# A diffusion layer with 32 experts: expert biases split behind the router, weight slots given back in two steps, waits moved in the expert loop

## The chip, the cores and the metric

The kernel runs on one core of one Trainium2 chip. TensorE (PE) does the matmuls, VectorE (DVE), ScalarE (ACT) and GpSimd (POOL) the elementwise work, and SyncE (SP) issues most DMAs. The metric is the device time of one execution, in microseconds (us): 1415.83 us before, the median of three runs from 1415.27 to 1415.89.

## The reference

One layer, 256 tokens of 1024 values. An adaLN-modulated bidirectional gated DeltaNet attention over the tokens and a context, then a mixture of 32 experts of which each token takes its best four, then an RMSNorm:

```python
hx2 = modulate(rmsnorm(x, norm2_g), mx[3], mx[4])
logits = hx2 @ w_r + b_r
top_v, top_i = lax.top_k(logits, 4)
comb = one_hot(top_i) weighted with softmax(top_v)
for e in range(32):
    gu = hx2 @ w_gu[e] + b_gu[e]                     # 1024 x 2048
    gate = minimum(gu[:, :1024], 7); up = clip(gu[:, 1024:], -7, 7)
    y += comb[:, e] * ((up + 1) * gate * sigmoid(1.702 * gate) @ w_dn[e] + b_dn[e])
x = x + mx[5] * y
return rmsnorm(x, final_g)
```

(Written shorter than the source.) All values are float32. An expert's weights are 8 MB for `w_gu` and 4 MB for `w_dn`, 402 MB for all 32, and each is read once.

## The kernel before

**Stages.** The attention with the adaLN products runs from 0 to about 420 us; its instructions are put in order by a scheduler from the table `ORDER`, whose entries name operations (`k`, `v`, `q`, `st`, `norm`, `wo`, `op`, `bias`, `issue`). The router follows until about 436.5 us, then the loop over 32 experts until 1406 us, then the last scatter, the norm and the output.

**Weights.** The experts' weights are cut into 192 pieces of 2 MB, six for each expert: four of `w_gu`, each with two of the eight k-steps, and two of `w_dn`. They pass through a ring of nine buffers, called slots. `issue(n)` starts the next n pieces on SP's queue (line 778); a piece can start when the slot that it takes has been read to the end by the matmuls. Nine pieces are issued ahead of the loop (two of them by `issue` in `ORDER`, seven in `issue(NR - NA)`).

**An expert.** Up to 64 tokens are gathered by a one-hot matmul into `hTe` (one gather per pair of experts, `gather4`). `first(e, ks)` does k-steps of the gate and up product: `gemm1` (line 992), started by `gbias` (line 984), a matmul with the expert's row of the bias in three bfloat16 parts (`bgu`, 96 rows: three times 32 experts). Then `swish` on DVE and ACT, `turn` (four transposes into `psT`, line 1010, and a copy to `aT` on ACT, line 1011), `dbias` (line 1018, with `bdn`), and the down product `gemm2r` (line 1025, 32 matmuls). For each pair, `weights` makes the matrix `ST` that scatters the outputs back, and `scatter` (line 1084) adds the pair before to the tokens. PE's order in the loop is the order in which the code is written. Before each `turn` PE runs k-steps 0 and 1 of the next expert.

**Overflow.** An expert with more than 64 tokens takes a second pass over the same weights in a block under `over()`, a branch on a flag that every engine loads after the router (`flag`, line 1122). In this run only expert 9 takes it. There are two such blocks for an expert: after the eight k-steps (line 1174) and after the down product (line 1204). Each is followed by `issue`: four slots after the first (one, one and two at three blocks for expert 0), two after the second. Where the branch isn't taken, SP's wait for a slot lasts until PE is past the branch. Another branch, `many` (line 1090), before expert 28, is for over 128 tokens and loads its number there.

**Biases.** `bias(i)` (line 835) splits a quarter of the biases into three bfloat16 parts, during the attention: casts on DVE (lines 844 and 846), subtracts on POOL (line 847).

Of the kernel before, what the change touches and what calls it, by code (L numbers as in the profile page):

```python
# [25 lines left out]
ORDER = [('k', 0), ('k', 1), ('ada',), ('n', 0), ('dc', 2), ('ada',), ('k', 2), ('dc', 1), ('ada',), ('ada',), ('dc', 0), ('k', 3), ('v', 1), ('um', 0), ('dc', 6), ('um', 1), ('ada',), ('n', 2), ('dc', 3), ('v', 0), ('um', 2), ('um', 3), ('k', 6), ('ia', 0), ('k', 5), ('dc', 5), ('dc', 4), ('k', 4), ('v', 2), ('ada',), ('k', 7), ('ib', 0), ('v', 3), ('n', 4), ('v', 4), ('dc', 7), ('n', 6), ('um', 7), ('um', 5), ('ic', 0), ('um', 6), ('um', 4), ('v', 5), ('ia', 4), ('ada',), ('ada',), ('v', 6), ('st', 0, 0, 0), ('ada',), ('st', 0, 1, 0), ('st', 0, 2, 0), ('v', 7), ('q', 0), ('ada',), ('st', 0, 3, 0), ('ada',), ('q', 1), ('q', 3), ('z', 3), ('am', 0), ('q', 2), ('am', 1), ('q', 6), ('z', 1), ('am', 3), ('ada',), ('ada',), ('am', 2), ('st', 1, 0, 0), ('st', 1, 1, 0), ('st', 1, 2, 0), ('ib', 4), ('ic', 4), ('q', 5), ('q', 4), ('ada',), ('st', 0, 0, 4), ('st', 0, 1, 4), ('st', 0, 2, 4), ('ada',), ('ada',), ('q', 7), ('st', 1, 3, 0), ('st', 0, 3, 4), ('am', 7), ('am', 5), ('z', 2), ('z', 5), ('z', 0), ('am', 4), ('z', 4), ('z', 7), ('z', 6), ('am', 6), ('norm', 0, 1), ('wo', 2), ('st', 1, 0, 4), ('hclose',), ('st', 1, 1, 4), ('g1',), ('moec',), ('norm', 0, 0), ('wo', 6), ('bias', 4), ('wo', 1), ('st', 1, 2, 4), ('issue',), ('wo', 0), ('wo', 3), ('st', 1, 3, 4), ('bias', 5), ('wo', 5), ('norm', 4, 1), ('op', 0, 1), ('issue',), ('op', 0, 0), ('bias', 0), ('wo', 7), ('norm', 4, 0), ('wo', 4), ('op', 4, 1), ('op', 4, 0), ('bias', 2), ('bias', 1), ('bias', 3), ('fin',)]  # L26
# [26 lines left out]
def tile_kernel(ctx: ExitStack, tc: tile.TileContext, A, out):  # L53
# [88 lines left out]
    nc.scalar.dma_start(rowG, A["norm2_g"].rearrange("o (q r) -> (o q) r", q=4))  # L142
# [242 lines left out]
    V.tensor_scalar(neg_eg, eg, -1.0, None, op0=ALU.mult)  # L385

# [414 lines left out]
    mk, bx = {}, []  # L801

    def moec():
# [17 lines left out]
        bx.extend(xp.tile([P, 512], F32, tag=t, name="bx", bufs=1) for t in "gu")  # L821
# [11 lines left out]
    def bias(i):  # L833

        g, n = divmod(i, 2)
        if not n:
            for n_ in range(2):
                b = A["moe_b_dn"][0] if g == 2 else A["moe_b_gu"][0][:, g * D:(g + 1) * D]
                nc.sync.dma_start(bx[n_][32 * g:32 * g + 32], b[:, n_ * 512:(n_ + 1) * 512])
        x = bx[n][32 * g:32 * g + 32]  # L840
        hi = (mk["bdn"] if g == 2 else mk["bgu"][:, g * D:(g + 1) * D])[:, n * 512:(n + 1) * 512]
        sb = wka.tile([P, 512], BF, tag="vT", name="sb", bufs=1)[32 * g:32 * g + 32]
        for u in range(3):
            V.tensor_copy(hi[32 * u:32 * u + 32], x)
            if u < 2:
                V.tensor_copy(sb, x)
                G.tensor_tensor(x, x, sb, op=ALU.subtract)

    ops = {"dc": decu, "moec": moec, "fin": moer, "g1": gates, "bias": bias, "k": key, "n": knorm, "v": value, "um": umats, "ia": inv_a, "ib": inv_b, "ic": inv_c, "st": step, "q": query,
# [29 lines left out]
    fwi = mc.tile([1, 2], I32, name="fwi")  # L879
    xTs = [mw.tile([P, 8, P], F32, tag="hTe", name="xT") for _ in range(2)]  # L880
# [183 lines left out]
    def weights(e, oh):  # L1064

        pt = px()
        for t in range(2):
            T.transpose(pt[:, t * P:(t + 1) * P], oh[:, t].bitcast(F32), ident)
        ST = mw.tile([P, 4, P], FR, tag="ST", name="ST", bufs=1)
# [3 lines left out]
        for t in range(2):  # L1073
            T.matmul(pt[:, 256:260], oh[:, t], chl[:, t, e:e + 2].rearrange("p e w -> p (e w)"), start=(t == 0), stop=(t == 1))
# [12 lines left out]
    def many(p):  # L1087

        n_max = nc.values_load(cnti[0:1, E:E + 1], min_val=0, max_val=256)
# [31 lines left out]
    softmax()  # L1121
    flag = [nc.values_load(fwi[0:1, i:i + 1], min_val=0, max_val=65535) for i in range(2)]
    live = {}

    def first(e, ks):
# [5 lines left out]
        for k in ks:  # L1131
            gemm1(e, k, ws[k], hT[:, k, e % 2 * 64:e % 2 * 64 + 64], pg, pu)

    def beside(e, k):

        nonlocal ST, cw
        if e % 2:
            if e + 1 < E and k in (3, 5):
                nxt = pairs[e // 2 + 1]
                gather4(nxt[0].bitcast(F32), P, nxt[1], k // 4)  # L1140
        elif k == 4 and e:
            for n in range(2):
                for t in range(2):
                    scatter(t, n)
        elif k == 5:
# [6 lines left out]
    for e in range(E):  # L1152
# [11 lines left out]
        for k0, k1 in ((0, 2), (2, 4), (4, 8)) if e == 0 else ((2, 8),):  # L1164
            for k in range(k0, k1):
# [3 lines left out]
            if k0 == 0 or e:  # L1169
                pgo, puo = pb(f"G{1 - odd}"), pb(f"U{1 - odd}")  # L1170
            if k1 == 4:
                S.activation(s2[:, 0, 0:1], epsc, AF.Silu)
            tc.no_sync_barrier()
            with over():
                if k0 == 0 or e:
# [13 lines left out]
        for n in range(2):  # L1189
# [4 lines left out]
        for r in range(8):  # L1194
            gemm2r(r, ws[8 + r], aT, py, e, odd)
        y = xp.tile([P, 512], F32, tag="u", name="y", bufs=1)
        V.scalar_tensor_tensor(y, py, cw[:, odd:odd + 1], gate[:, odd], op0=ALU.mult, op1=ALU.mult)  # L1197
        for half in range(2):
            n = half ^ odd
            r = slice(64 * half, 64 * half + 64)  # L1200
            S.copy(YAB[0][r, n], y[r])  # L1201
# [59 lines left out]
```

## Time and profile before

| | |
|---|---|
| time, median of 3 runs | 1415.83 us (1415.27 to 1415.89) |
| the profiled execution | 1424.81 us |
| its span in the trace | 1423.0 us |
| PE busy | 1270.0 us, 89% |
| DVE, ACT, POOL busy | 501.1, 356.8, 229.6 us |
| mean DMA rate over the span | 321 GB/s |
| DMA rate in most slices of the expert loop | 426 to 428 GB/s |
| PE's clock in the loop, share of full speed | 0.96 to 1.00 |

The profile shows one execution. PE is busy nearly throughout, but a busy engine need not be the bound: in the expert loop the DMA rate stands at one value in most slices, and falls in three: at the loop's start, around 740 us and shortly after 1297 us. The columns of the DMA rate in windows of the trace therefore belong beside PE's busy time. The profiled execution took 8.98 us more than the median of the runs.

### The profile page before, as it was taken

Reading aid. Unit: us, or ns where it says so; the run is one execution under the profiler, and the core shown is the slowest. Engines: PE = TensorE matmul, PEld = TensorE weight load, DVE = VectorE, ACT = ScalarE, POOL = GpSimd, SP = SyncE. Lnnn points to the kernel's source line nnn. Section 1 sums busy time; section 2 is a strip of 40 time slices with the busy share of each in tenths; the row PEclk is TensorE's granted clock in tenths of the full one; section 3 lists DMA queues with packets and bytes.
Section 4 is the critical chain, followed back from the end, with each engine's and each line's share of the span. In section 5 each row is a group of like instructions: output and inputs, shape, how many; then the busy total and the mean of one; then the engine's idle time right before and its main releaser. Section 6 shows DMA issues by size and latency. Waiting matters only on the chain. (4 is left out here: it accounts for less than half of the span.)

```text
span 1423.0 us, 18206 instructions
## 1 busy us (share of the span) xinstructions
PE 1270.0 (89%) x6815; PEld 642.7 (45%) x6815; DVE 501.1 (35%) x1101; ACT 356.8 (25%) x802; POOL 229.6 (16%) x216
## 2 busy tenths in 40 slices
PE   4999889999889999999998999999889899897995
PEld 2576677688544433434333433334334344342432
DVE  4569988866762112021112112121120211212022
ACT  3366443455323111111111111111111111110112
POOL 3043234334430100011000110001000010000011
PEclk9899999989999999999999999999999999999996
DMA  9632433443577899999984999999999999999991
GB/s 257 190 117 81 119 104 105 149 134 115 168 299 313 330 428 425 427 426 426 427 343 191 428 426 426 427 427 426 427 426 426 427 426 427 427 421 378 430 426 51
DMA packets 88432, 456.27 MB, mean 321 GB/s; under 512 B 7892, under 2 KB 57241, under 8 KB 63713
## 3 DMA queue, kind: packets, MB, share of 16 engines
q1 hardware_dynamic: 85680, 454.08, 79.5%
q8 instruction: 93, 1.52, 0.4%
q10 hardware_dynamic: 2609, 0.26, 0.2%
q14 instruction: 50, 0.41, 0.1%
HBM read 453.27 MB, written 1.05 MB: 319 GB/s over the span
## 5 line engine op out<-in xcount | busy, mean ns | idle before, releaser
L992 PE MATMUL psG<-w,hTe 128*64 128x512 f32 x1024 | 282.3, 607 | 30.6 <-DMA w<-in_moe_w_gu_dram 18.2
L992 PE MATMUL psU<-w,hTe 128*64 128x512 f32 x1024 | 277.2, 597 | 0.0
L1025 PE MATMUL psY<-w,aT 128*64 128x512 f32 x1024 | 229.2, 600 | 22.0 <-ACT aT L1011 22.0
L1202 POOL TENSOR_TENSOR YAB<-y,YAB 64x512 fp32r<-64x512 f32 x62 | 79.6, 1283 | 891.7 <-ACT YAB L1201 889.4
L1197 DVE SCALAR_TENSOR_TENSOR y<-psY,cw,gate 128x512 f32<-128x512 f32 x32 | 24.0, 751 | 373.5 <-PE psY L1025 373.5
L992 PEld LDWEIGHTS psU<-w,hTe 128*64 128x64 f32 x1024 | 89.0, 138 | 127.6 <-issue 115.3
L1025 PEld LDWEIGHTS psY<-w,aT 128*64 128x64 f32 x1024 | 71.2, 138 | 159.5 <-issue 129.8
L992 PEld LDWEIGHTS psG<-w,hTe 128*64 128x64 f32 x1024 | 77.6, 137 | 141.3 <-issue 114.3
L1000 DVE TENSOR_SCALAR g<-psG 128x512 f32<-128x512 f32 x33 | 34.4, 1041 | 260.2 <-PE psG L992 260.0
L1201 ACT CAST YAB<-y 64x512 fp32r<-64x512 f32 x64 | 39.4, 616 | 259.2 <-DVE y L1197 137.9
L268 PE MATMUL pp<-hh,w 128*128 128x256 f32 (+1 forms) x240 | 86.2, 373 | 5.9 <-DVE acc L443 4.4
L269 PE MATMUL pp<-hl,w 128*128 128x256 f32 (+1 forms) x240 | 84.8, 367 | 0.0
L977 ACT ACTIVATE hTe<-psX,adac,A 128x128 f32<-128x128 f32 x128 | 48.3, 457 | 116.2 <-PE psX L975 116.2
L83 POOL TENSOR_TENSOR w<-w 128x1024 fp32r<-128x1024 f32 x24 | 57.5, 2396 | 105.6 <-ACT w L78 32.3
L1029 DVE TENSOR_TENSOR x<-x,psX 128x512 f32<-128x512 f32 x68 | 43.9, 685 | 83.0 <-PE psX L1084 81.1
L975 PEld LDWEIGHTS psX<-oh,xn 128*128 128x128 f32 x512 | 59.5, 191 | 25.0 <-issue 25.0
L975 PE MATMUL psX<-oh,xn 128*128 128x128 f32 x512 | 65.4, 281 | 0.6 <-DVE oh L966 0.6
L443 DVE SCALAR_TENSOR_TENSOR acc<-pp,colB,acc 128x508 f32<-128x508 f32 (+3 forms) x96 | 62.4, 653 | 9.4 <-ACT acc L431 8.5
L1011 ACT ACTIVATE aT<-psT 128x512 f32<-128x512 f32 x32 | 19.1, 597 | 157.8 <-PE psT L1010 157.8
L268 PEld LDWEIGHTS pp<-hh,w 128*128 128x128 f32 x240 | 49.8, 208 | 18.5 <-issue 3.6
L269 PEld LDWEIGHTS pp<-hl,w 128*128 128x128 f32 x240 | 50.1, 209 | 6.4 <-issue 1.0
L424 PE MATMUL pp<-hh,w 128*128 128x256 f32 (+1 forms) x240 | 52.3, 349 | 0.0
(394 smaller groups left out, 1458.7 us busy)
## 6 DMA issues: line engine op xcount, KB each, us to landing
w<-in_moe_w_gu_dram SPq DMA_DIRECT2D x128, 2048.0 KB, 24.5
w<-in_moe_w_dn_dram SPq DMA_DIRECT2D x64, 2048.0 KB, 20.2
w<-in_gdn_w_in_dram SPq DMA_DIRECT2D x32, 512.0 KB, 4.0
w<-in_ada_w_dram SPq DMA_DIRECT2D x32, 512.0 KB, 4.0
sl<-in_ada_w_dram SPq DMA_DIRECT2D x16, 512.0 KB, 5.7
w<-in_gdn_w_out_dram SPq DMA_DIRECT2D x8, 512.0 KB
xt<-in_ctx_dram SPq DMA_DIRECT2D x2, 512.0 KB
xt<-in_x_dram SPq DMA_DIRECT2D x2, 512.0 KB
```

The costliest lines, as they stand in the source:

```text
L83: eng[e2].tensor_tensor(lo, x, hi.bitcast(F32), op=ALU.subtract)
L268: T.matmul(ps, wh, xh, start=first, stop=False)
L269: T.matmul(ps, wh, xl, start=False, stop=last and not low)
L424: T.matmul(p[:, t0:512], w[1][:, k], hh[:, k, t0:512], start=False, stop=(k == 7))
L443: V.scalar_tensor_tensor(o, i, tap(j), o, op0=ALU.mult, op1=ALU.add)
L975: T.matmul(pt[:, d % 4 * n:d % 4 * n + n], xn[:, t, d * P:(d + 1) * P], oh[:, t, 0:n], start=(t == 0), stop=(t == 1))
L977: S.activation(dst[:, d, 0:n], pt[:, d % 4 * n:d % 4 * n + n], AF.Identity, scale=A2[:, d:d + 1], bias=B2[:, d:d + 1])
L992: T.matmul(ps[64 * c:64 * c + 64], hc, w[:, q * D + c * 512:q * D + (c + 1) * 512], start=False, stop=(k == 7))
L1025: T.matmul(py[o:o + 64], aT[:, b, c * 64:(c + 1) * 64], w[:, n * 512:(n + 1) * 512], start=False, stop=(r == 7))
L1029: V.tensor_tensor(xs, xs, ps, op=ALU.add)
L1201: S.copy(YAB[0][r, n], y[r])
L1202: (G if e + 1 < E else V).tensor_tensor(YAB[1][r, n], y[r], YAB[0][r, n].bitcast(F32), op=ALU.subtract)
```

## The change

1. `bias` leaves `ORDER`. It is written again behind the router, for three biases instead of six quarters: for each, ACT's queue issues three copies of 128 KB (32 rows of 1024) into a 96-row tile, ACT casts (once 96 rows, three times 32), DVE subtracts twice. Two tiles are used in turn. Expert 0 adds `gbias` behind its last k-step instead of ahead of its first (`late`).
2. The row of `norm2_g` is loaded and transposed at the end of the gates' stage instead of the kernel's start.
3. The block under `over()` behind the k-steps is split in two for each expert (after k-step 3 and after k-step 7), each followed by `issue(2)`; for expert 0 in four, each with `issue(1)`.
4. In the loop: only k-step 0 of the next expert stands ahead of `turn`, k-step 1 and `dbias` behind it; `weights` runs at k-step 6 instead of 5 and puts its small matmuls with `chl` ahead of ACT's casts; `scatter` is halved between k-steps 3 and 5; the odd expert's `gather4` stands at k-steps 2 and 5 instead of 3 and 5.
5. The number for `many` is loaded once, with the flags.
6. For the last expert the second overflow block stands ahead of the down product, and a small Sqrt activation (it brings the function table) behind its `turn`.

```diff
-ORDER = [... ('bias', 4) ... ('bias', 5) ... ('bias', 0) ... ('bias', 2), ('bias', 1), ('bias', 3), ('fin',)]
+ORDER = [... ('fin',)]
...
+    def bias(i):
+        x = mw.tile([P, D], F32, tag=f"YAB{i % 2}", name="bx", bufs=1)[0:96]
+        hi = bdn if i == 2 else bgu[:, i * D:(i + 1) * D]
+        b = A["moe_b_dn"][0] if i == 2 else A["moe_b_gu"][0][:, i * D:(i + 1) * D]
+        for u in range(3):
+            nc.scalar.dma_start(x[32 * u:32 * u + 32], b)
+        S.copy(hi, x)
+        V.tensor_tensor(x, x, hi, op=ALU.subtract)
+        for u in (1, 2):
+            S.copy(hi[32 * u:32 * u + 32], x[32 * u:32 * u + 32])
+        V.tensor_tensor(x[64:96], x[64:96], hi[64:96], op=ALU.subtract)
+        S.copy(hi[64:96], x[64:96])
...
+    for i in range(3):
+        bias(i)
     flag = [nc.values_load(fwi[0:1, i:i + 1], min_val=0, max_val=65535) for i in range(2)]
+    n_max = nc.values_load(cnti[0:1, E:E + 1], min_val=0, max_val=256)
...
-        for k0, k1 in ((0, 2), (2, 4), (4, 8)) if e == 0 else ((2, 8),):
-            for k in range(k0, k1):
+        done = 0
+        for k1 in ((2, 4, 6, 8) if e == 0 else (4, 8)):
+            for k in range(max(done, 2) if e else done, k1):
                 first(e, [k])
                 beside(e, k)
...
-                for k in range(k0 if e == 0 else 0, k1):
-                    gemm1(e, k, ws[k], hco[:, k], pgo, puo)
+                for k in range(done, k1):
+                    gemm1(e, k, ws[k], hco[:, k], pgo, puo, e == 0)
...
-            issue((k1 - (k0 if e == 0 else 0)) // 2)
+            issue((k1 - done) // 2)
+            done = k1
         u = swish(pg, pu)
         if e + 1 < E:
-            first(e + 1, (0, 1))
-        py = pb("Y")
-        for n in range(2):
-            dbias(e, n, py[64 * (n ^ odd):64 * (n ^ odd) + 64])
+            first(e + 1, [0])
         aT = turn(u, act("aT"))
+        if e + 1 < E:
+            first(e + 1, [1])
+        else:
+            S.activation(sf[:, 0, 3:4], aT[:, 0, 0:1], AF.Sqrt, scale=0.0, bias=epsc)
```

Line numbers of the changed kernel are some two to twelve higher from the expert loop's helpers on.

On SP, the last five of the nine pieces that are issued ahead of the loop (pieces 4 to 8). `DMAHW0` to `DMAHW7` are eight completion counters that the DMAs of all queues take in turn; a DMA waits for the earlier one that had its counter. Before:

```order
L778 DMA w<-in_moe_w_dn_dram 128x4096 [waits DMAHW7_49,DVE_49,Activation_49]
L778 DMA w<-in_moe_w_dn_dram 128x4096 [waits DMAHW0_49,DVE_49]
L778 DMA w<-in_moe_w_gu_dram 128x4096 [waits DMAHW1_49,PE_49]
L778 DMA w<-in_moe_w_gu_dram 128x4096 [waits DMAHW2_49]
L778 DMA w<-in_moe_w_gu_dram 128x4096 [waits DMAHW3_49,DVE_49]
```

In the changed kernel:

```order
L780 DMA w<-in_moe_w_dn_dram 128x4096 [waits DMAHW3_49,DVE_49,Activation_49]
L780 DMA w<-in_moe_w_dn_dram 128x4096 [waits DMAHW7_49,DVE_49]
L780 DMA w<-in_moe_w_gu_dram 128x4096 [waits DMAHW1_49,PE_49]
L780 DMA w<-in_moe_w_gu_dram 128x4096 [waits DMAHW4_49]
L780 DMA w<-in_moe_w_gu_dram 128x4096 [waits DMAHW6_49,DVE_49]
```

The nine bias copies take their turns among these DMAs. Counter 4 was last taken by the third bias copy and counter 6 by the fifth, so that pieces 7 and 8 stand behind the landing of those copies, where they stood behind older transfers.

On ACT, from the gather for expert 0 (`hTe`) to the scatter matrix `ST` of the first pair; `fwi` is the flag word, `s` from `epsc` is the small activation that brings the Silu table. Before:

```order
L977 ACTIVATE hTe<-psX,adac,A_3486 128x128 x4
L1122 TENSOR_LOAD fwi x2
L1174 REGISTER_ALU
L1174 COMPARE_AND_BRANCH
L977 ACTIVATE ho<-psX,adac,A_3486 128x64 x8
L1174 UNCONDITIONAL_BRANCH x2
L1172 ACT_TABLE_LOAD
L1172 ACTIVATE s_3843<-epsc 128x1
L1174 REGISTER_ALU
L1174 COMPARE_AND_BRANCH
L1174 UNCONDITIONAL_BRANCH x2
L1070 CAST ST<-psX 128x256
```

In the changed kernel, of the same place (behind the last row shown come three more casts for `bdn`, the loads and the branch):

```order
L979 ACTIVATE hTe<-psX,adac,A_3487 128x128 x4
L930 DMA bx<-in_moe_b_gu_dram 32x1024 x3
L931 CAST bgu<-bx 96x1024
L930 DMA bx<-in_moe_b_gu_dram 32x1024
L934 CAST bgu<-bx 32x1024 x2
L931 CAST bgu<-bx 96x1024
L936 CAST bgu<-bx 32x1024
L934 CAST bgu<-bx 32x1024 x2
L930 DMA bx<-in_moe_b_dn_dram 32x1024
L936 CAST bgu<-bx 32x1024
L930 DMA bx<-in_moe_b_dn_dram 32x1024 x2
L931 CAST bdn<-bx 96x1024
```

Between the gather and the flag loads there are now twelve casts and seven of the nine copies (the first stands ahead of the gather, the second within it); the Silu table and `ST` come after them.

On PE, expert 0's turn and down product, with the end of the k-steps of expert 1 that stand ahead. Before:

```order
L992 MATMUL psU_4247<-w,hTe 64x512
L992 MATMUL psG_4246<-w,hTe 64x512 x2
L992 MATMUL psU_4247<-w,hTe 64x512 x2
L1018 LDWEIGHTS sel_3457
L1018 MATMUL psY<-bdn,sel_3457 64x512
L1018 LDWEIGHTS sel_3457
L1018 MATMUL psY<-bdn,sel_3457 64x512
L1010 MATMUL psT<-ident,u 128x128 [waits DVE_49,PE_49]
L1010 MATMUL psT<-ident,u 128x128 x3
L1025 MATMUL psY<-w,aT 64x512 [waits DMAHW7_49,Activation_49]
L1025 MATMUL psY<-w,aT 64x512 x7
```

In the changed kernel:

```order
L995 MATMUL psU_4252<-w,hTe 64x512
L1015 MATMUL psT<-ident,u 128x128 [waits DVE_49,PE_49]
L1015 MATMUL psT<-ident,u 128x128 x3
L995 MATMUL psG_4251<-w,hTe 64x512 x2
L995 MATMUL psU_4252<-w,hTe 64x512 x2
L1023 LDWEIGHTS sel_3458
L1023 MATMUL psY<-bdn,sel_3458 64x512
L1023 LDWEIGHTS sel_3458
L1023 MATMUL psY<-bdn,sel_3458 64x512
L1030 MATMUL psY<-w,aT 64x512 [waits DMAHW3_49,Activation_49]
L1030 MATMUL psY<-w,aT 64x512 x7
```

The four transposes into `psT` have moved ahead of k-step 1 of the next expert and of the two `dbias` matmuls, which now stand between them and the first matmul that reads `aT`.

## Rows read from the trace of the kernel before

**Rows 1.** Windows: stretch, length, busy (x count) of five engines, clock, DMA share, GB/s.

```profile
436.50:484.00 47.50, 44.52 (x223) 18.95 (x223) 7.90 (x17) 10.32 (x23) 2.57 (x2) 1.00 0.71 273
484.00:717.00 233.00, 216.02 (x1059) 91.55 (x1057) 40.29 (x72) 38.12 (x83) 20.50 (x16) 1.00 1.01 426
717.00:777.50 60.50, 53.71 (x240) 18.46 (x238) 16.33 (x29) 5.69 (x11) 2.58 (x2) 0.97 0.59 239
...
1297.50:1315.00 17.50, 15.80 (x70) 5.82 (x68) 5.93 (x11) 1.74 (x4) 0.00 (x0) 0.96 0.85 333
```

**Rows 2.** SP timeline, experts 0 to 2: start, length, queue, line, operation, transfer, count.

```profile
440.74 0.33 SPq L778 DMA_DIRECT2D w<-in_moe_w_gu_dram  x1
...
454.21 0.33 SPq L778 DMA_DIRECT2D w<-in_moe_w_dn_dram  x1
...
467.01 0.81 SPq L778 DMA_DIRECT2D w<-in_moe_w_gu_dram  x2
...
481.96 0.34 SPq L778 DMA_DIRECT2D w<-in_moe_w_gu_dram  x1
...
538.38 0.33 SPq L778 DMA_DIRECT2D w<-in_moe_w_gu_dram  x1
```

**Rows 3.** PE's waits: tile and line, what ended them, us in total, times, longest.

```profile
PE psY L1025 <- ACT aT L1011: 22.0, 32, 0.7
PE psX L1074 <- ACTq L1174: 19.5, 16, 1.2
...
PE psG L992 <- PEq L1090: 7.2, 1, 7.2
PE psG L984 <- PEq L1174: 4.8, 30, 0.2
```

**Rows 4.** PE timeline, end of attention: start, us, line, operation [idle before, releaser].

```profile
372.33 1.12 PE L704 MATMUL pm<-row,ident 128*128 128x512 f32 x2 [3.46 <-DVE St L664]
...
407.60 0.30 PE L729 MATMUL pt<-ident,o 128*128 128x128 f32 x1 [0.96 <-DVE kT L730]
```

**Rows 5.** DVE timeline of the same stretch, one row.

```profile
388.74 3.12 DVE L844 CAST bgu<-bx 32x512 bf16<-32x512 f32 x3
```

**Rows 6.** ACT timeline, expert 0: the Silu table.

```profile
438.27 1.28 ACT L1172 ACT_TABLE_LOAD   x1
```

**Rows 7.** DMA issues: transfer, queue, count, KB each, median us to landing.

```profile
out_dram<-xn SPq DMA_DIRECT2D x4, 256.0 KB, 3.8
...
rowB<-in_gdn_conv_w_dram ACTq DMA_DIRECT2D x1, 60.0 KB, 6.1
```

**Rows 8.** ACT by line and form: count, busy us, mean ns, idle before.

```profile
L78 ACT CAST w<-w 128x1024 fp32r<-128x1024 f32 x13 | 13.6, 1047 | 2.2 <-POOL w L83 2.2
```

**Rows 9.** DVE by line and form.

```profile
L83 DVE TENSOR_TENSOR w<-w 128x1024 fp32r<-128x1024 f32 x6 | 7.6, 1264 | 0.1
```

**Rows 10.** PE timeline, expert 0: first weight matmul, turn, down product.

```profile
436.55 0.64 PE L992 MATMUL psG<-w,hTe 128*64 128x512 f32 x1
...
458.45 0.66 PE L1010 MATMUL psT<-ident,u 128*128 128x128 f32 x4
...
459.79 7.09 PE L1025 MATMUL psY<-w,aT 128*64 128x512 f32 x32 [0.69 <-ACT aT L1011]
```

**Rows 11.** PE timeline, last expert.

```profile
1391.06 1.06 PE L992 MATMUL psU<-w,hTe 128*64 128x512 f32 x4
...
1396.45 9.45 PE L1025 MATMUL psY<-w,aT 128*64 128x512 f32 x32 [0.69 <-ACT aT L1011]
```

**Rows 12.** SP timeline around expert 9's overflow.

```profile
719.24 0.33 SPq L778 DMA_DIRECT2D w<-in_moe_w_gu_dram  x1
...
751.25 0.33 SPq L778 DMA_DIRECT2D w<-in_moe_w_gu_dram  x1
...
774.93 0.33 SPq L778 DMA_DIRECT2D w<-in_moe_w_gu_dram  x1
```

**Rows 13.** PE timeline around expert 9's overflow.

```profile
759.23 1.08 PE L992 MATMUL psG<-w,hTe 128*64 128x512 f32 x4
```

More of the change, by code (lines that the diff above doesn't have):

```diff
@@ L385, in tile_kernel @@
     V.tensor_scalar(neg_eg, eg, -1.0, None, op0=ALU.mult)
+    nc.scalar.dma_start(rowG, A["norm2_g"].rearrange("o (q r) -> (o q) r", q=4))
+    pt = pT()
+    for a in range(2):
+        T.transpose(pt[:, 4 * a:4 * a + 4], rowG.rearrange("q (p a) -> q a p", a=2)[:, a], ident[0:4, 0:4])
+    S.copy(colA[:, 25:33].rearrange("p (q a) -> p a q", a=2), pt[:, 0:8].rearrange("p (a q) -> p a q", a=2))
     ectx.close()
@@ L800, in tile_kernel @@
     E = 32
-    mk, bx = {}, []
+    mk = {}
     def moec():
@@ L820, in moec @@
         xt("A2", [P, 8])
-        bx.extend(xp.tile([P, 512], F32, tag=t, name="bx", bufs=1) for t in "gu")
+        for t in "gu":
+            xp.tile([P, 512], F32, tag=t, name="bx", bufs=1)
     def moer():
@@ L831, in moer @@
         V.tensor_tensor(mk["wr"], mk["wr"], mk["A2"].rearrange("p (k e) -> p k e", e=1).to_broadcast([P, 8, E]), op=ALU.mult)
[L833 to L849, printed above, removed]
+    ops = {"dc": decu, "moec": moec, "fin": moer, "g1": gates, "k": key, "n": knorm, "v": value, "um": umats, "ia": inv_a, "ib": inv_b, "ic": inv_c, "st": step, "q": query,
            "am": amats, "z": zgate, "ada": lambda: next(ag, None), "hclose": hclose, "norm": norm, "wo": wo, "op": oproj,
@@ L1068, in weights @@
             T.transpose(pt[:, t * P:(t + 1) * P], oh[:, t].bitcast(F32), ident)
+        for t in range(2):
+            T.matmul(pt[:, 256:260], oh[:, t], chl[:, t, e:e + 2].rearrange("p e w -> p (e w)"), start=(t == 0), stop=(t == 1))
         ST = mw.tile([P, 4, P], FR, tag="ST", name="ST", bufs=1)
@@ L1137, in beside @@
         if e % 2:
-            if e + 1 < E and k in (3, 5):
+            if e + 1 < E and k in (2, 5):
                 nxt = pairs[e // 2 + 1]
                 gather4(nxt[0].bitcast(F32), P, nxt[1], k // 4)
-        elif k == 4 and e:
-            for n in range(2):
-                for t in range(2):
-                    scatter(t, n)
-        elif k == 5:
+        elif k in (3, 5) and e:
+            for t in range(2):
+                scatter(t, k // 4)
+        elif k == 6:
             ST, cw = weights(e, pairs[e // 2][0])
@@ L1182, in tile_kernel, with down @@
             tc.no_sync_barrier()
-            issue((k1 - (k0 if e == 0 else 0)) // 2)
+            issue((k1 - done) // 2)
+            done = k1
         u = swish(pg, pu)
         if e + 1 < E:
-            first(e + 1, (0, 1))
-        py = pb("Y")
-        for n in range(2):
-            dbias(e, n, py[64 * (n ^ odd):64 * (n ^ odd) + 64])
+            first(e + 1, [0])
         aT = turn(u, act("aT"))
+        if e + 1 < E:
+            first(e + 1, [1])
+        else:
+            S.activation(sf[:, 0, 3:4], aT[:, 0, 0:1], AF.Sqrt, scale=0.0, bias=epsc)
         if not odd:
             YAB = [mw.tile([P, 2, 512], FR, tag=f"YAB{i}", name="YAB", bufs=1) for i in range(2)]
[L1194 to L1201, printed above, removed]
-            (G if e + 1 < E else V).tensor_tensor(YAB[1][r, n], y[r], YAB[0][r, n].bitcast(F32), op=ALU.subtract)
+        def down():
+            py = pb("Y")
+            for n in range(2):
+                dbias(e, n, py[64 * (n ^ odd):64 * (n ^ odd) + 64])
+            for r in range(8):
+                gemm2r(r, ws[8 + r], aT, py, e, odd)
+            y = xp.tile([P, 512], F32, tag="u", name="y", bufs=1)
+            V.scalar_tensor_tensor(y, py, cw[:, odd:odd + 1], gate[:, odd], op0=ALU.mult, op1=ALU.mult)
+            for half in range(2):
+                n = half ^ odd
+                r = slice(64 * half, 64 * half + 64)
+                S.copy(YAB[0][r, n], y[r])
+                (G if e + 1 < E else V).tensor_tensor(YAB[1][r, n], y[r], YAB[0][r, n].bitcast(F32), op=ALU.subtract)
+        if e + 1 < E:
+            down()
         tc.no_sync_barrier()
@@ L1212, in tile_kernel @@
         issue(2)
+        if e + 1 == E:
+            down()
     pe.close()
-    sf = mc.tile([P, 2, 4], F32, name="sf")
-    S.activation(sf[:, 0, 3:4], aT[:, 0, 0:1], AF.Sqrt, scale=0.0, bias=epsc)
     fg = mw.tile([P, D], F32, tag="hTe", name="fg")
```

30 lines of the change are left out of this document (13 added, 17 removed).

## The prediction

> **What bounds the kernel now.** I read the windows first. In the loop's undisturbed stretch, 484 to 717 us, the DMA engines move 426 GB/s without a break, though PE is busy only 216 of 233 us [rows 1]. A piece of 2.097 MB thus takes 4.92 us, the six of an expert 29.5 us, and the 192 pieces 945 us of a loop of some 970. Then the issues on SP: the first piece that goes out behind an even and an odd expert's k-steps starts at 481.96 and, two experts on, at 538.38 [rows 2], so PE needs 56.42 / 2 = 28.2 us per expert when it isn't held up. The stream is the bound, by 1.3 us per expert, and the question for each edit is whether the stream moves when it now stands still. The time lost in a stretch is its length times (1 - rate/426): 47.5 x (1 - 273/426) = 17.1 us at the loop's start, 60.5 x (1 - 239/426) = 26.6 us around expert 9's overflow, 17.5 x (1 - 333/426) = 3.8 us behind the branch at expert 28 [rows 1]. Third come PE's waits: 22.0 us for `aT`, 19.5 us for the scatter matrix, one of 7.2 us at the rare branch, and 4.8 us over 30 branches that are not taken [rows 3]. Ahead of the loop no stream counts but PE's chain, and there I read PE's idle time and what ended it.
>
> **The change part by part, on the profiled execution's clock** (1424.81 us, 8.98 above the median of the runs; the sum is taken off both).
>
> *Biases out of the attention.* DVE is the engine that PE waits for at the attention's end: six waits from 3.46 us at 372.33 to 0.96 us at 407.60, 9.4 us together [rows 4]. Among DVE's work there stand bias casts, three of them 3.12 us in one go just ahead of a small operation that PE's chain needs [rows 5]. Without them I take two thirds of the 9.4, -6.5 us. The ends are -10 (all of it) and +3.5: the scheduler orders the whole stage anew, and may lay a wait such as the longest here somewhere else. Moving the row of `norm2_g` costs one small DMA and two transposes beside other work: 0, and at most one of the short waits, 1 us, if the transposes hold PE.
>
> *Bias preparation behind the router: the first lost time.* Before, two of the nine early pieces keep the stream busy into the loop, and the first returned slot goes out at 440.74 [rows 2]. By the order, piece 7 now waits for the third bias copy, which ACT issues behind the gather's eight activations. Before, those are done just ahead of the Silu table load at 438.27 [rows 6], so the copy goes out at about 438.6. No row has such a copy: the nearest are 3.8 us for 256 KB on SP's queue and 6.1 us for 60 KB on ACT's [rows 7]. I take 3.8, as the copy's rows are whole ones and the stream is then empty, so piece 7 starts at 442.4. The stream runs dry 2 x 4.92 = 9.8 us earlier and restarts 1.7 later: +11.5. With 6.1 it is 2.3 more.
>
> *The second lost time.* Now slots come back at each second k-step, and pieces 7 to 12 go out in one train. Before, returns at 440.74, 454.21, 467.01 and 481.96 with two pieces of work (9.84 us) in each distance of 12.8 to 15 us [rows 2] left holes of 3.5, 3.0 and 5.1 us. The first two holes close: -6.5. The third gets longer, because the chain of casts holds ACT. Cast 1.05 us, subtract 1.26 us [rows 8, 9]: from 442.4 the first two biases, interleaved as the order has them, take to 453.9; the third one's copies need the first one's tile, go out until 454.6 and land at 458.4; then 1.05 + 1.26 + 2 x 1.05 + 1.26 + 1.05 = 6.7, to 465.1. The Silu table (1.28 us, hidden before, now on the path [rows 6]), the scatter casts, Silu and the product on DVE follow, some 5 us. The turn of expert 0 stands at 470.3, before at 458.45 [rows 10], 12 us later. PE has nothing else there, since only k-step 0 of expert 1 is ahead of the turn. Its 32 down matmuls then take 7.09, or 9.45 as for the last expert behind a wait [rows 10, 11], and the two slots come back at about 482.5. The train of six pieces ends at 443.4 + 29.5 = 472.9, so the hole is 10.6 instead of 5.1 us: +5.5. Start in all: 11.5 - 6.5 + 5.5 = +10.5. Ends: -6 (only the closed holes, if nothing of the preparation shows) and +20 (slower copies, and again behind pieces).
>
> *Waits in the loop.* Each expert loses the 0.69 us for `aT`, each even one the 1.22 us ahead of the `chl` matmuls [rows 3], and gains a branch of 4.8/30 = 0.16 us. PE falls from 28.2 to about 26.9 us per expert. Under a stream of 29.5 this pays nothing: PE waits 2.6 us for weights instead. It pays where PE is behind.
>
> *Overflow of expert 9.* The four slots that come back from 719.24 on [rows 12] come earlier, but the stream still has pieces then, so this pays nothing. The fifth comes back at 751.25, inside the second block; with PE's wait for `aT` and as much again less ahead of it, 1.35 us earlier. Two pieces last until about 762; the next slot returns only at 774.93 [rows 12], after all k-steps of expert 10: 13 of the 26.6 us are lost there. These k-steps start at 759.23 [rows 13]. In the new order two slots return after k-steps 2 and 3, 16 matmuls (3.4 us: four take 1.08 us [rows 13], of which some 0.2 overlap the next four), and half the scatter (1.1): 759.23 - 1.35 + 3.4 + 1.1 = 762.4. That is 12.5 us earlier, and the two further slots follow before these pieces are through. -1.35 - 12.4 = -13.7, with -10 if small holes between single returns stay.
>
> *Rare branch.* The load is some 0.3 us of the 7.2; the rest stays. But two slots come back half an expert earlier, and the hole of 3.8 us [rows 1] closes: -3.8 (0 if it doesn't).
>
> *End.* The last k-steps are through at 1391.06 + 1.06, the down product at 1405.9 [rows 11]. The branch at 28 held PE for 7.2 us and the stream for 3.8, so PE is late there; it now gains 3 x 1.3 = 3.9 us over three experts. Of this I take 2.7, the rest being the stream's own end; ends 0 and -5. The second block's place and the early Sqrt table change a not-taken branch and 1.28 us beside other work: 0, at most -1.3.
>
> Sum: -6.5 + 10.5 - 13.7 - 3.8 - 2.7 = -16.2; 1424.81 becomes 1408.6, the median 1415.83 becomes **1399.6**.
>
> **The rivals.** *A, the preparation costs nothing:* copies land at once and PE's turn has other cover. For it speaks that 1.15 MB are only 2.7 us of stream; against it, ACT's fixed order. The term is -6 instead of +10.5: 1383.
>
> *B, the copies stand behind pieces:* the last three go out while the train of pieces runs. If they wait for two pieces, 9.84 us, the turn and the second hole move by as much: 1409.4. The 6.1 us of [rows 7] on ACT's queue speak a little for it. The Trainium skill ("DMA: Bandwidth & Descriptors", section "Queues, rings and completion order") says that each DMA engine goes round the queues that have work, packet by packet; by this the copies would not wait for whole pieces, and the sum stays at the forecast's. No row here shows two queues in contest.
>
> *C, slower: a branch more per expert costs what the rare branch costs.* Expert 28's took 7.2 us, though it isn't entered [rows 3]: PE goes on at a far place of its program. If the new split does this for each of 31 experts, PE needs 26.9 + 7.0 = 33.9 us, 4.4 above the stream: +136, 1536. It decides from 2.6 us per branch on, and outweighs the gains from 2.6 + 16.2/31 = 3.1. Against it: 30 branches of the same kind cost 0.16 us [rows 3], while `many` jumps over 32 experts' code. The Trainium skill ("Runtime: NRT & Kernel Launch", section "Instruction fetch mechanics") has the rule that speaks for C: a taken branch whose target lies outside the window already fetched must wait for a fetch. The trace agrees at expert 28, 7.2 us, and not at the others.
>
> *D, the split gives nothing at the overflow,* because slots come back singly there already, or SP is held elsewhere: without the 13.7, 1413.3.
>
> **How the numbers follow.** A difference within 0.2%, 2.8 us, can't be told from none. Forecast 0.60 with its own range 1391 to 1408; A 0.12; B 0.11; C 0.07; D 0.10. Faster (below 1413.0): 0.54 of the forecast's, A, 0.08 of B, 0.05 of D, 0.79. Same: 0.03 + 0.02 + 0.04, 0.09. Slower (above 1418.7): C's 0.07, 0.03 of a forecast with a bad reordering, 0.02 of B and D, 0.12. The range is 1384 to 1414: from nearly A to D; C and the outermost of the rest stay out.
>
> **What would show it.** Expert 0's first matmul some 6 us earlier; piece 7 on SP at 442 less that shift, just after a bias copy's landing; a PE wait of about 12 us ahead of expert 0's turn, caused by ACT or DVE; a lost time of some 27 us at the start and 13 around the overflow, where the rate no longer stays away for over 10 us; no dip behind expert 28; the waits for `aT` and `chl` gone, and some 2.6 us of waits for weights per expert in their place. The prediction is wrong if the turn isn't late (A), if the copies take over 8 us (B), if PE waits at the new branches for microseconds (C), or if the overflow still loses over 20 us (D).

## The result, and the profile after

| | before | after |
|---|---|---|
| median (range) | 1415.86 us (1412.89 to 1418.92, 6 runs) | 1423.68 us (1418.68 to 1426.26, 6 runs) |
| ratio, 95% interval | 1 | 1.0052 (1.0028 to 1.0075) |
| profiled execution | 1424.81 us, span 1423.0 | 1418.68 us, span 1416.9 |

The changed kernel is slower by 0.5%, about 7.4 us; 1399.6 us was forecast. The two profiled executions stand the other way round: that of before lies above all six of its timed runs, that of after is the fastest of its six. So the profiles are compared here stretch by stretch, and sums are taken from ratios (0.01 of a ratio is 14.2 us). A second profile of the changed kernel (`again`) shows where executions of one program differ: expert 0 starts at 437.4 instead of 434.4 us, but from its first down product to the end there are 941.2 us in the one and 941.3 in the other. Of the 3.5 us between the two, 3.1 arise ahead of the loop.

The loop did most of what was forecast. The windows of [rows 1] in the changed kernel (stretch, length, busy of five engines, clock, DMA share, GB/s):

```profile
436.50:484.00 47.50, 28.84 (x128) 10.12 (x126) 11.48 (x14) 16.79 (x20) 0.00 (x0) 0.82 0.77 284
484.00:717.00 233.00, 221.01 (x1075) 89.32 (x1071) 42.64 (x75) 38.69 (x84) 22.77 (x18) 0.99 1.00 425
717.00:777.50 60.50, 55.69 (x270) 20.65 (x269) 11.78 (x20) 7.62 (x18) 2.52 (x2) 1.00 0.78 322
1297.50:1315.00 17.50, 16.16 (x72) 6.28 (x68) 5.85 (x11) 1.73 (x4) 0.00 (x0) 0.95 1.01 424
```

Behind the branch at 28 0.1 us of the stream are lost instead of 3.8. Around expert 9's overflow the window gives 60.5 x (1 - 322/426) = 14.8 us instead of 26.6, but the changed kernel's hole comes later and outlasts the window. Up to 800 us, changed kernel and then before:

```profile
717.00:800.00 83.00, 77.23 (x378) 29.59 (x379) 17.10 (x30) 11.27 (x26) 5.05 (x4) 1.00 0.83 339
```

```profile
717.00:800.00 83.00, 75.36 (x354) 28.11 (x352) 17.08 (x30) 10.02 (x21) 5.15 (x4) 0.98 0.70 290
```

So 17.0 us are lost there instead of 26.5. In the first window PE is busy 28.84 us instead of 44.52, at a clock of 0.82. PE's waits, as in [rows 3]:

```profile
PE psG L995 <- DMA w<-in_moe_w_gu_dram: 25.0, 10, 4.0
PE psX L1073 <- ACTq L1181: 17.4, 1, 17.4
...
PE psG L995 <- PEq L1094: 6.8, 1, 6.8
PE psG L986 <- PEq L1181: 5.1, 30, 0.5
...
PE psG L995 <- PEq L1181: 3.6, 19, 0.3
```

The waits for `aT` and, on the even experts, for the `chl` matmuls are gone. New is one of 17.4 us. PE's timeline shows its place (start, us, line, operation, what the engine waited for):

```profile
434.36 1.08 PE L995 MATMUL psG<-w,hTe 128*64 128x512 f32 x4
...
465.59 0.69 PE L1073 MATMUL psX<-ident,oh 128*128 128x128 f32 x2 [17.42 <-ACTq L1181]
...
466.43 1.98 PE L995 MATMUL psG<-w,hTe 128*64 128x512 f32 x4
...
472.98 0.66 PE L1015 MATMUL psT<-ident,u 128*128 128x128 f32 x4
...
475.56 7.04 PE L1030 MATMUL psY<-w,aT 128*64 128x512 f32 x32
```

Expert 0's turn comes 38.6 us behind its first matmul, in [rows 10] 21.9. But PE is not held at the turn: it stands at the transposes for the scatter matrix, k-step 6, until ACT is past a branch (L1181). ACT's timeline says what ACT did (its first row is the third copy's issue):

```profile
434.48 0.32 ACTq L930 DMA_DIRECT2D bx<-in_moe_b_gu_dram  x1
...
448.28 1.04 ACT L936 CAST bgu<-bx 32x1024 bf16<-32x1024 f32 x1 [1.28 <-DVE bx L935]
448.29 0.79 ACTq L930 DMA_DIRECT2D bx<-in_moe_b_dn_dram  x2
458.29 1.04 ACT L931 CAST bdn<-bx 96x1024 bf16<-96x1024 f32 x1 [8.97 <-DMA bx<-in_moe_b_dn_dram]
460.63 2.10 ACT L934 CAST bdn<-bx 32x1024 bf16<-32x1024 f32 x2 [1.29 <-DVE bx L932]
464.01 1.04 ACT L936 CAST bdn<-bx 32x1024 bf16<-32x1024 f32 x1 [1.28 <-DVE bx L935]
465.60 1.28 ACT L1179 ACT_TABLE_LOAD   x1 [0.55 <-ACTq L1181]
```

The last copies go out at 448.29 and the first cast that reads them starts at 458.29; the chain ends at 465.05, and PE goes on at 465.59. On SP, piece 7 goes out at 436.74, 2.4 us behind expert 0's first matmul, and after the long wait the next slots come back at 470.67 and 482.72 (SP's timeline, as [rows 2]):

```profile
436.74 0.33 SPq L780 DMA_DIRECT2D w<-in_moe_w_gu_dram  x1
...
470.67 0.34 SPq L780 DMA_DIRECT2D w<-in_moe_w_gu_dram  x1
...
482.72 0.33 SPq L780 DMA_DIRECT2D w<-in_moe_w_gu_dram  x1
```

From the first down product on, the loop takes 1416.9 - 475.56 = 941.3 us, before 1423.0 - 459.79 = 963.2 [rows 10]: 21.9 gained. The start takes 18.0 more (475.56 - 434.36 = 41.2 against 23.2), so that from expert 0's first matmul to the end 3.9 us are gained in all. Expert 0 begins at 434.36 instead of 436.55. That the median is nevertheless higher points ahead of the loop.

### The profile page after: what moved, and what is told of

Its sections match the earlier page's. It is cut to its first block, busy times and chain, and to the rows that moved or that the text cites. A ratio compares the mean times of both kernels' runs of the same rounds, so it can differ in the third digit from the quotient of the medians.

```text
span 1416.9 us, 18778 instructions
## 1 busy us (share of the span) xinstructions
PE 1269.2 (90%) x6815; PEld 629.3 (44%) x6815; DVE 497.9 (35%) x1076; ACT 363.7 (26%) x811; POOL 214.5 (15%) x204
## 5 line engine op out<-in xcount | busy, mean ns | idle before, releaser
L1030 PE MATMUL psY<-w,aT 128*64 128x512 f32 x1024 | 225.2, 592 | 0.1
L995 PEld LDWEIGHTS psU<-w,hTe 128*64 128x64 f32 x1024 | 85.4, 141 | 134.6 <-issue 131.6
L995 PEld LDWEIGHTS psG<-w,hTe 128*64 128x64 f32 x1024 | 66.7, 137 | 147.6 <-issue 109.9
L264 PE MATMUL pp<-hh,w 128*128 128x256 f32 (+1 forms) x240 | 86.6, 376 | 13.1 <-DVE w L78 5.1
L1077 ACT CAST ST<-psX 128x256 fp32r<-128x256 f32 x16 | 5.9, 371 | 170.0 <-PE psX L1075 170.0
```

The costliest lines, as they stand in the source:

```text
L264: T.matmul(ps, wh, xh, start=first, stop=False)
L1030: T.matmul(py[o:o + 64], aT[:, b, c * 64:(c + 1) * 64], w[:, n * 512:(n + 1) * 512], start=False, stop=(r == 7))
```

## The experiments

All ratios are to the kernel before, with 95% intervals. "Start" is expert 0's first weight matmul, "first product" the first matmul of its down product, both from PE's timeline of the run's profile. The expectations of the first set count to the end of the down product, 7.0 us later.

**First set: the bias preparation or the loop?**

`again`, the changed kernel unaltered. 

> The changed kernel once more, beside the runs below on one chip. Theory S (the bias preparation behind the router holds the start of the loop, by 16 to 18 us at expert 0's down product in the trace, and this outweighs what the loop gains): ratio 1.003 to 1.008 as measured, with expert 0's down product about 48 us behind its first weight matmul (30.3 before). Theory L (the loop itself got worse, because PE now waits for weights and its clock falls): the same ratio, but the loss spread over the experts.

Measured: 1.0062 (1.0037 to 1.0088). First product 41.8 us behind the start.

`oldbias_newloop`:

```diff
 # the changed kernel, with before's ORDER, bias(i) in the attention, no late
-    for i in range(3):
-        bias(i)
```

> The changed kernel with the bias preparation back in the attention stage, as before. Theory S: expert 0's down product within 31 us of its first weight matmul, lost stream time at the start about 11 to 17 us, around the overflow about 15, none behind expert 28; in all 12 to 18 us faster than the kernel before (ratio 0.987 to 0.992). Theory L: as slow as the changed kernel or at best equal to the kernel before (1.000 to 1.008).

Measured: 0.9983 (0.9963 to 1.0003). First product 22.3 us behind the start, 941.1 us from there to the end. But the start is at 452.6. The stream's windows from the start to 500 us, here and then before:

```profile
452.60:500.00 47.40, 45.21 (x225) 18.62 (x225) 7.91 (x17) 10.35 (x24) 2.58 (x2) 1.00 0.84 339
```

```profile
436.50:500.00 63.50, 59.67 (x293) 24.61 (x291) 9.14 (x20) 12.15 (x26) 5.14 (x4) 1.00 0.78 310
```

`newbias_oldloop`:

```diff
 # the kernel before, with the changed ORDER and late
+    for i in range(3):
+        bias(i)
```

> The kernel before with the bias preparation moved behind the router alone (expert 0's bias matmuls last, as in the changed kernel; the loop as before). Theory S: slower than the kernel before by 10 to 18 us (1.007 to 1.013), with PE held 15 us or more in expert 0. Theory L: within 0.2% of the kernel before, the delay being taken up by the loop's slack.

Measured: 1.0085 (1.0060 to 1.0109). First product 47.0 us behind the start, 963.2 us from there. Start at 416.1.

`nobias`, the changed kernel without the preparation:

```diff
     def bias(i):
+        if i == 0:
+            G.memset(bgu, 0.0); G.memset(bdn, 0.0)
-        x = mw.tile(...)    # copies, casts and subtracts
```

> The changed kernel without the bias preparation: the biases are left out, bgu and bdn are cleared once by POOL (so the experts' biases are missing from the result). Theory S: faster than the kernel before by 15 to 22 us (0.985 to 0.990), a few us faster still than with the preparation in the attention stage, by what the attention's DVE is freed of. Theory L: as slow as the changed kernel, 1.003 to 1.008.

Measured: 0.9929 (0.9902 to 0.9955); 21.9 us to the first product, start at 442.0.

What follows: the loop's gain is real and always nearly the same, 963.2 us against 941 to 943; theory L falls. The preparation costs what theory S says, 1.0062 - 0.9929 = 1.3% or 19 us. But S alone is too little: without the preparation behind the router, `oldbias_newloop` gains hardly anything, because its attention ends 16 us later than before's in the two profiles. In `newbias_oldloop` expert 0's first product comes 23.7 us later behind the start than before, and the last expert's still 22.9: the old loop makes up for none of it. The four starts fall into two pairs: with the row of `norm2_g` at the kernel's start 436.6 and 416.1, with the row moved 452.6 and 434.4.

**Second set: the moved row.**

`rowg_back`:

```diff
 # the changed kernel
+    nc.scalar.dma_start(rowG, ...)              # at the start again, with its
+    T.transpose(...); V.tensor_copy(colA[:, 25:33], ...)   # transposes and copy
...
-    nc.scalar.dma_start(rowG, ...)              # end of the gates' stage
-    pt = pT(); T.transpose(...); S.copy(colA[:, 25:33], ...)
```

> The changed kernel with the row of norm2_g back at the kernel's start, all else as changed. Theory R (moving that row's transposes into the gates' stage makes the scheduler order the attention anew, and this costs some 20 us, which the traces so far show only as different starts of expert 0: 452.6 and 434.4 with the row moved, 436.6 and 416.1 with it at the start): expert 0 starts at about 416 us, the time falls by 18 to 22 us against the changed kernel, ratio to the kernel before 0.989 to 0.993. Rival V (those starts differ from execution to execution): expert 0 at 430 to 437 and the ratio 1.002 to 1.008, as changed.

Measured: 0.9891 (0.9873 to 0.9908), median 1401.49 us; start at 413.4. V falls.

`rowg_moved`: the opposite edit in the kernel before. 

> The kernel before with that row alone moved to the gates' stage. Theory R: expert 0 starts at about 450 us, slower than the kernel before by 16 to 23 us, ratio 1.011 to 1.016. Rival V: within 0.2%.

Measured: 1.0121 (1.0102 to 1.0139), start at 450.4. The moved row costs 1.2% alone, 17 us, and 1.0062 - 0.9891 = 1.7%, 24 us, in the changed kernel. PE has the same work up to expert 0 in `rowg_back` and in the changed kernel; the windows of the two, in this order:

```profile
0.00:413.40 413.40, 371.66 (x2603) 272.62 (x2603) 303.12 (x757) 201.51 (x475) 131.96 (x139) 0.96 0.50 157
```

```profile
0.00:434.40 434.40, 377.43 (x2605) 279.67 (x2605) 309.83 (x756) 196.56 (x472) 131.89 (x139) 0.94 0.48 150
```

PE idles 41.7 us in the one and 57.0 in the other, and its 2603 and 2605 matmuls take 5.8 us longer at a clock of 0.94 instead of 0.96. The difference is not in one place: in 300 to 350 us, for instance, PE does 466 matmuls in the one and 345 in the other, where a wait for ACT's casts of a weight tile stands (PE's timeline, changed kernel):

```profile
310.52 0.58 PE L264 MATMUL pp<-hh,w 128*128 128x256 f32 x1 [3.00 <-ACT w L78]
```

`rowg_dummy`:

```diff
 # rowg_back, and in the gates' stage once more, without the load
+    pt = pT(); T.transpose(...); S.copy(colA[:, 25:33], ...)
```

> The changed kernel with the row loaded and transposed at the start, and the two transposes and ACT's copy in the gates' stage done as well (the same values a second time; only the late load is gone). If it is the transposes, the buffer and the copy in that stage that shift the order of what follows: as slow as the changed kernel, 1.003 to 1.008, expert 0 at 434 to 440. If it was the late load that held somebody up: as the kernel with the row back at the start, 0.989 to 0.993.

Measured: 1.0028 (1.0007 to 1.0049), start at 437.7: not the late load.

`rowg_nopt`:

```diff
 # the changed kernel
-    pt = pT()
-    T.transpose(pt[:, 4 * a:4 * a + 4], ...)
+    T.transpose(pt[:, 128 + 4 * a:132 + 4 * a], ...)   # the buffer of the stage's last transpose
```

> The changed kernel with the row's two transposes in free columns of the last buffer of the gates' stage instead of a PSUM buffer of their own; load, transposes and ACT's copy stay there. If the buffer taken out of the rotation is what shifts the attention: as with the row at the start, expert 0 at about 415 us, 0.987 to 0.992. If it is ACT's copy and the transposes in the order: as changed, expert 0 at 434 to 440, 1.002 to 1.008.

Measured: 1.0029 (1.0008 to 1.0050), start at 431.5: not the buffer either.

`rowg_dve`:

```diff
 # the changed kernel
-    S.copy(colA[:, 25:33], ...)
+    V.tensor_copy(colA[:, 25:33], ...)
```

> The changed kernel with the row's copy in the gates' stage on DVE instead of ACT. If ACT's copy in that place is what holds the attention up: expert 0 starts at about 415 us, ratio 0.987 to 0.993. If any instruction put in there makes the scheduler order what follows anew, and the order table fits only the old set of instructions: again slower than with the row at the start, expert 0 somewhere between 420 and 440, 0.993 to 1.008.

Measured: 1.0080 (1.0041 to 1.0118), start at 444.3: not ACT's copy.

`rowg_life`:

```diff
 # rowg_back, and in the gates' stage
+    T.transpose(pt[:, 128 + 4 * a:132 + 4 * a], ...)   # nobody reads it
```

> The changed kernel with the row loaded, transposed and copied at the start as before, and nothing more in the gates' stage than the two transposes once again, into columns that nobody reads (no load, no copy, no buffer). If PE's two transposes there are enough to shift the order: expert 0 at 420 to 440, 0.993 to 1.008. If it takes the copy behind them: as with the row at the start, 0.987 to 0.993.

Measured: 1.0079 (1.0053 to 1.0104), start at 440.4. Two transposes of four columns, read by nobody, cost 1.0079 - 0.9891 = 1.9%. In all kernels that put something into that stage the start lies between 431 and 444; in those that leave it alone between 413 and 420 (the biases being out of the attention in both). What changes is the order that the scheduler makes of everything behind. PE's timelines show the place, `rowg_back` first and then the changed kernel:

```profile
75.26 1.44 PE L424 MATMUL pp<-hh,w 128*128 128x512 f32 x5
76.53 0.27 PE L457 MATMUL pt<-ident,kT 128*128 128x128 f32 x1
76.56 0.48 PE L424 MATMUL pp<-hh,w 128*128 128x512 f32 x1
```

```profile
76.49 0.40 PE L386 MATMUL pt<-ident,rowG 4*128 4x4 f32 x2
...
77.57 1.90 PE L426 MATMUL pp<-hh,w 128*128 128x512 f32 x7
79.31 0.27 PE L459 MATMUL pt<-ident,kT 128*128 128x128 f32 x1
79.33 0.46 PE L501 MATMUL pm<-nsel,gj 128*128 128x512 f32 x1
```

Up to the row's transposes PE has the same order in both, right behind them the orders part. Take the matmuls up to expert 0, with neighbours of one source line and the same tiles counted as one group: of `rowg_back`'s 914 groups 704 come in the same order in the changed kernel, but 911 in the kernel before and all 914 in `newbias_oldloop` and `owntile`. `again` and `nobias` have the changed kernel's order in every group, `rowg_dummy`, `rowg_nopt` and `rowg_moved` in all but a few; `rowg_dve` and `rowg_life` have others. So taking the biases out left PE's order as it was, and what goes into the gates' stage makes a new one. Which of the displaced instructions costs the time is left open.

**Third set: the start.**

`owntile`:

```diff
 # rowg_back
+    parts = [bias(i) for i in range(4)]      # copies only, ahead of the gather;
     gather(pairs[0][0].bitcast(F32), P, pairs[0][1])   # bdn in halves, tiles "aT", "ho"
...
+    for b_ in parts:
+        bsplit(*b_)                          # casts and subtracts
```

> The kernel with the row back at the start, and the bias copies changed: all are issued before the gather for expert 0, and the down bias goes in two halves into tiles of its own, so that no copy waits for a tile or lands behind weight pieces. Theory S with that wait (9.0 us before the third bias's first cast, in the 17.4 us that PE is held in expert 0): PE's wait in expert 0 falls to 6 to 10 us and the time by 5 to 10 us against the kernel with the row back, ratio 0.983 to 0.988. If the chain of casts alone holds PE, or copies ahead of the gather delay it as much: within 3 us of that kernel.

Measured: 0.9857 (0.9837 to 0.9876), median 1396.25 us; PE's wait in expert 0 is 5.4 us (18.2 in `rowg_back`), first product 29.2 us behind the start (42.2). The gather's results come later: 1.69 us of wait ahead of expert 0.

```profile
419.81 1.08 PE L1002 MATMUL psG<-w,hTe 128*64 128x512 f32 x4 [1.69 <-ACT hTe L986]
...
438.98 0.69 PE L1080 MATMUL psX<-ident,oh 128*128 128x128 f32 x2 [5.36 <-ACTq L1189]
```

The wait fell by 12.8 us, the time by 5. Behind the first product 3.4 us are lost again (945.3 instead of 942.0), and expert 0 starts 6.4 us later than in `rowg_back` (419.8, 413.4). That wait of 1.69 is a part of it; how much of the rest the copies cost, and how much is the spread of executions, isn't shown.

`owntile2`:

```diff
 # owntile
-            nc.scalar.dma_start(x[32 * u:32 * u + 32], b)
+            nc.gpsimd.dma_start(x[32 * u:32 * u + 32], b)
-        S.copy(hi, x) ...
+        V.tensor_copy(hi, x) ...             # for bdn's halves
```

> The kernel with early copies and tiles of their own for the down bias (0.9857), with two more edits: the copies go through POOL's queue instead of ACT's, and the down bias is cast by DVE instead of ACT. If ACT's work (copies ahead of the gather, then casts) is what still holds expert 0: PE's wait there falls from 5.4 to about 2 us or less, expert 0's first matmul moves 2 to 4 us ahead, the time 3 to 7 us below it (0.981 to 0.984). If POOL's copies start later than ACT's or the stream sets the end of the start: within 2 us of it.

Measured: 0.9826 (0.9796 to 0.9856), median 1393.17 us, the fastest of all; its interval still meets `owntile`'s. The mechanism expected is not seen: PE's wait is 8.2 us, the start 419.1. Why it is faster, if it is, stays open.

**Fourth set: the two parts of the loop**, both from `rowg_back` (0.9891).

`onestep`:

```diff
-        for k1 in ((2, 4, 6, 8) if e == 0 else (4, 8)):
+        for k1 in ((2, 4, 6, 8) if e == 0 else (8,)):
```

> The kernel with the row of norm2_g back at the start (0.9891 of the kernel before), and from expert 1 on one overflow block after all eight k-steps again, four slots given back at once. If the two-step return is what the loop gains by: lost stream time around the overflow back from about 13 to 25 us, a hole of some 4 us behind expert 28, and the time 10 to 17 us above the kernel with the row back (0.996 to 1.001). If the removed waits make the gain: within 3 us of it (0.987 to 0.992).

Measured: 0.9975 (0.9955 to 0.9995), 11.9 us slower. The hole behind the branch at 28 is back: windows of `onestep`, then of `rowg_back`:

```profile
466.00:698.00 232.00, 220.17 (x1050) 87.52 (x1050) 42.62 (x75) 37.65 (x81) 22.49 (x18) 0.98 0.99 417
698.00:780.00 82.00, 76.22 (x376) 29.60 (x374) 16.69 (x30) 10.39 (x25) 2.53 (x2) 1.00 0.77 316
1293.00:1310.00 17.00, 15.81 (x75) 6.09 (x77) 5.85 (x11) 2.33 (x5) 0.00 (x0) 1.00 0.85 344
```

```profile
466.00:698.00 232.00, 221.77 (x1069) 89.22 (x1068) 42.65 (x75) 38.90 (x84) 21.12 (x17) 0.99 1.01 426
698.00:780.00 82.00, 76.38 (x371) 28.96 (x371) 17.08 (x30) 10.45 (x24) 5.04 (x4) 1.00 0.82 337
1293.00:1310.00 17.00, 15.80 (x84) 6.56 (x82) 2.79 (x4) 3.46 (x7) 2.53 (x2) 1.00 1.00 422
```

Lost time in the three: 4.9, 21.2 and 3.3 us against 0, 17.1 and 0.2. So 4 us at the overflow hang on the two steps, 5 behind the start, 3 at the branch.

`oldwaits`:

```diff
-            first(e + 1, [0])
+            first(e + 1, (0, 1)); py = pb("Y"); dbias(...)
         aT = turn(u, act("aT"))
-            first(e + 1, [1])
 # and weights at k-step 5 with chl behind the casts, scatter at 4, gathers at 3 and 5
```

> The kernel with the row back at the start, and the loop's order as before the change: both k-steps and the down bias ahead of the turn, the weights with the chl matmuls behind ACT's casts at k-step 5, the scatter whole at k-step 4, the gathers at 3 and 5; the two-step return stays. By the prediction's step (these waits lie under the stream) the time is within 3 us of the kernel with the row back (0.987 to 0.992), with PE's waits for weights some 1.1 us less per expert. If PE's pace counts: 6 to 15 us slower (0.993 to 1.000).

Measured: 0.9989 (0.9974 to 1.0005), 13.9 us slower: the removed waits count. PE's waits of `oldwaits`:

```profile
PE psY L1028 <- ACT aT L1014: 21.3, 31, 0.7
PE psX L1071 <- ACTq L1180: 20.9, 1, 20.9
PE psX L1077 <- ACTq L1180: 20.2, 16, 1.9
```

The first product stands 47.2 us behind the start instead of 42.2: the transposes for the scatter matrix come one k-step earlier here, so that PE is held with more of expert 0 still to do. From the first product it takes 952.7 us instead of 942.0. Counted from the start, `oldwaits` is 5.0 us behind `rowg_back` at expert 0's first product, 14.4 at expert 15's, but only 8.6 at expert 27's and 15.7 at the end. Much of what PE falls behind in the middle thus costs nothing in the end, because `rowg_back` waits for weights there. What stays is the 5.0, some 4 at the overflow (21.3 us of the stream lost from 698 to 800, against 17.0), and 7 behind expert 27.

## Why the prediction was wrong

**The step that failed** is the last sentence on the attention: moving the row "costs one small DMA and two transposes beside other work: 0, and at most one of the short waits, 1 us". It costs 17 us alone and 24 in the changed kernel. The sentence before it names the mechanism ("the scheduler orders the whole stage anew") but charges it, at most +3.5, to the removed biases only, and the row was priced by its instructions. The runs show the reverse: without the biases PE's order stays, with the row moved it is another. With that row back, all other edits in, the kernel takes 1401.49 us (0.9891), 1.9 above the forecast of 1399.6. In that set the kernel before took 1418.15; by the ratio it is 1400.4, 0.8 above.

The traces put the miss in the same place. From expert 0's first matmul to the end the changed kernel gains 3.9 us, where 9.7 were forecast (+10.5 - 13.7 - 3.8 - 2.7); the median is 7.4 higher, so what lies ahead of the loop costs 11 where -6.5 was forecast. The agreement of `rowg_back` with the forecast is luck in part, as errors cancel: of its 15.4 us (by the ratio) the loop gains 2.3 (984.2 against 986.5), 7.4 less than forecast, and the attention 13.1, 6.6 more. Term by term:

- *Biases out of the attention*, -6.5 with an end at -10. In `newbias_oldloop` the preparation's move costs 0.85%, 12.0 us, and its start 47.0 - 23.2 = 23.8 us more; -11.8 are left for the attention. `again` against `oldbias_newloop` gives 11.2 - 19.0 = -7.8. Right in sign, somewhat small. The new order of the stage that was feared for this edit came with the row.
- *The start*, +10.5, is 11.5 + 5.5 = 17.0 for the preparation and -6.5 for two closed holes. `nobias` measures 19 for the preparation. The holes close without it: `oldbias_newloop` loses 47.4 x (1 - 339/426) = 9.7 us of the stream from the start to 500, before 63.5 x (1 - 310/426) = 17.3, so -7.6. The sum is nearly right, its parts are not. The third copy, issued at 434.48, lets piece 7 out at 436.74, so that it landed within 2.3 us, not 3.8. The down bias's copies go out 13.8 us behind it (448.29), not 16.0 (454.6 - 438.6), but need some 10 us to land, not 3.8; the chain ends 30.6 us behind it instead of 26.5. And PE is caught at the scatter transposes, two k-steps ahead of the turn. (The forecast lets the train of pieces start at 443.4; its hole of 10.6 us goes by 442.4, the time that it gives for piece 7.) This is rival B's mechanism, in one place and with its 9.84 us. By the Trainium skill's packet by packet rule ("DMA: Bandwidth & Descriptors", section "Queues, rings and completion order") the copies wouldn't wait for whole pieces; the trace has them land after 10.0 us, about two pieces' time, with five pieces issued since 436.74, so that it bears out the rule only in that they didn't wait for all.
- *Overflow, branch and end*, -13.7, -3.8 and -2.7. At the overflow 17.0 us are lost (13 forecast), 9.5 less than before. The forecast counts PE's 1.35 twice there, as the 762.4 for the next slot already holds it; with one of the two edits alone, in `onestep` and in `oldwaits`, the traces lose 21.3 each (698 to 800 us). At the branch the loss falls by 3.7, and from the last expert's k-steps on the end is 0.5 + 2.8 us shorter.
- *Waits in the loop* were let pay 1.35 us at the overflow and 2.7 at the end, and nothing elsewhere "under a stream of 29.5". `oldwaits` loses 13.9: 5.0 in expert 0, where none was forecast, some 4 at the overflow, 7 behind expert 27. From expert 0's to expert 5's first product PE needs 27.2 us per expert, before 28.1 (26.9 and 28.2 in the forecast, which left out the added branch's 0.16); the wait for weights that was to fill 2.6 us per expert is 25.0 us in all, in ten places, the first at 635 us. That the loop came out near its sum all the same is because the two-step return brings 11.9, not its 17.5 (13.7 + 3.8). The two don't overlap: 25.8 apart, 27.5 for the whole loop (`newbias_oldloop` 1.0085 against `rowg_back` 0.9891, which have the same attention and preparation).

Of the rivals, C falls: the branches behind the k-steps hold PE for 5.1 us in 30 places and 3.6 in 19, 0.17 and 0.19 each. D is right in part: of 12.4 us forecast for the split at the overflow, 4 hang on it in `onestep`. A falls: the preparation costs 19.

## What to carry to other kernels

In a stage whose order comes from a scheduler and a table tuned for one set of instructions, an edit that looks small can reorder everything behind it: price an added or moved instruction there by a measurement of that stage, with a range of its own on both sides, and try each such edit alone. Work moved from a busy stage to a quiet one is paid by whoever joins its engine's queue: follow that queue to the first branch or buffer that another engine waits for. When a gain is called hidden under a transfer, look up in which stretches the transfer is really what is waited for.

## What the hardware showed that was not expected

A copy of 128 KB on ACT's queue landed within 2.3 us (434.48 to 436.74) with the stream nearly idle (144 GB/s from 434.0 to 436.7) and took about 10 us with weight pieces in flight. The same program's executions differ by up to 16 us (before: 1409.23 to 1425.05 in 10 runs); in the two profiles of the changed kernel nearly all of their difference lies ahead of the expert loop. In the window from 436.5 to 484, which holds PE's wait of 17.4 us, the mean clock was 0.82: behind the wait, from 466.4 to 469.0, it was 0.50, the lower of the clock's two levels (1.2 GHz), and four matmuls at 466.43 took 1.98 us, against 1.08 at 434.36; from 470.0 to 475.5 it was 1.00 again.
